# Reordering the first two experts of a mixture-of-experts layer, with an early load of ScalarE's Silu table

## The chip, the cores and the metric

One core of a Trainium2 chip runs the whole program. The metric is the device time of one execution, in microseconds. The program uses TensorE (PE in the profile, PEld for its weight loads), VectorE (DVE), ScalarE (ACT), GpSimd (POOL) and the queues that issue transfers, SyncE's (SP) above all.

## What is computed

One layer: a bidirectional gated linear attention (GLA) over 512 latent tokens with a 256-token context prefix, then a top-2 mixture of 16 experts, then a norm. Cut to what matters here:

```python
x = x + g1 * gla_mixer(modulate(rmsnorm(x), sh1, sc1), ...)
# inside the mixer: the gates of both directions
logdecay = log_sigmoid(z) / 16
# the mixture
scores = sigmoid(h @ w_router)
for e in range(16):
    he = silu(h @ w1[e]) * (h @ w3[e])
    out = out + gates[:, e:e + 1] * (he @ w2[e])
x = x + g2 * out
return rmsnorm(x, final_g)
```

The norms take 1/sqrt through a logarithm and an exponential (`rsqrt`, L139 and L140), and log_sigmoid is made from an absolute value, an exponential and a logarithm (`gate`, L369 to L371).

## The kernel before, in words

The attention part comes first. `rsqrt` normalizes three row blocks of the input (u = 0, 1, 2); TensorE transposes them (L202). Then `proj` runs five projections: for each, weights arrive in the `st` buffers, ScalarE casts them to a rounded copy `wh` (L281), VectorE subtracts to get the rest `wl` (L282), and TensorE does three matmuls per product (`mm3`, L51 to L53). During two of the projections a background generator `gates` is advanced. Each of its 12 steps is a TensorE matmul into a bank of the two-bank pool `pb` (L380 or L385), three ScalarE activations on one tile (L369 Abs, L370 Exp, L371 Ln) and a VectorE operation (L372) that reads the bank again and thereby frees it. So a step's matmul waits for the L372 of the step two before it.

Functions of ScalarE come in table sets. The program's builder puts a table load (ACT_TABLE_LOAD) in front of every activation whose function is not in the set loaded last, and `S.preload_act_table_set` asks for a set by hand. L60 asks for one with both Exp and Ln at the start of the program; L585 and L590 switch for Tanh and back; L1152, the first Silu, has a load in front of it.

Then the output projection, the second norm and the routing: VectorE forms the residual rows (L722, L723), TensorE transposes them (L730) and multiplies the router's weights (L737), and VectorE picks groups, ranks tokens and writes the order of the experts, `eid`, at L1057 (`eidl`). Gate weights are computed on GpSimd by `weights()` (L1083 to L1095) and copied by ScalarE (L1096).

The experts follow in a fixed list `order`; expert 0 is the class `First`, whose rows are collected by a matmul, expert 1 is a `Tile_`, whose rows GpSimd gathers (L1107). `up` computes gate and up products in two halves "a" and "b", `act` the Silu, `tr` and `dn` the down projection, `store` the scaled result, `scatter` the add into memory. `conv` splits weights (ScalarE L56, VectorE L57, 128x1024 each). `release` gives weight buffers back and `pump` issues the next expert's loads on SP.

Who sets the order: outside `manual_schedule` blocks a scheduler places each engine's instructions. In the main loop of the experts only GpSimd (`G.engine`) keeps the written order; TensorE, VectorE and ScalarE are scheduled. `tc.issue_after(ins)` adds an order edge to `ins` for those instructions of its block that run on the engine of `ins`. The weight splits of expert 1's half "a" carry such edges behind `scored[0]` (ScalarE, L909) and `eidl` (VectorE, L1057), at L1258 to L1260. Instructions that need no data and carry no edge can be placed at any point.

Of the kernel before, what the change touches and what calls it, by code (L numbers as in the profile page):

```python
# [32 lines left out]
def dit_kernel(ctx: ExitStack, tc: tile.TileContext, I, out):  # L33
    nc = tc.nc
    V, S, G, PE = nc.vector, nc.scalar, nc.gpsimd, nc.tensor
# [14 lines left out]
    def mm3(o, ah, al, bh, bl, first, last):  # L50
        PE.matmul(o, ah, bh, start=first, stop=False)  # L51
        PE.matmul(o, ah, bl, start=False, stop=False)  # L52
        return PE.matmul(o, al, bh, start=False, stop=last)  # L53
# [136 lines left out]
    for u in range(3):  # L190
# [5 lines left out]
        for k2 in range(4):  # L196
            pt = bank()
            ptv = pt.rearrange("p (k t) -> p k t", k=2)
            for k in range(2):
                for n in range(2):  # L200
                    kt = 2 * k2 + k
# [74 lines left out]
    def conv(st):  # L276
        w = cvs.pop(0)
        cvs.append(w)
        if halves[0]:
            for k in range(2):  # L280
                S.copy(w[0][:, k], st[:, k])  # L281
                mark[0] = V.tensor_sub(w[1][:, k], st[:, k], w[0][:, k].bitcast(F32))  # L282
        else:
            mark[0] = split(w[0], w[1], st)
        return w
# [394 lines left out]
    wts = [{} for _ in range(NE)]  # L680
# [23 lines left out]
    def release(u, *us):  # L704
        free.extend(u.pop(s) for s in us)
        pump()
# [39 lines left out]
    for k2 in range(4):  # L746
        w = first[k2] if k2 < 2 else wconv(2 * k2)
# [11 lines left out]
    w = [wconv(8), wconv(10)]  # L759
# [314 lines left out]
    def ranked():  # L1074
        zz = big1[:, 0:4 * ND * ND].rearrange("p (t a b) -> p t a b", t=4, a=ND)
        V.tensor_mul(zz, zk.unsqueeze(2).to_broadcast([P, 4, ND, ND]), perm.unsqueeze(1).to_broadcast([P, 4, ND, ND]))
        V.tensor_reduce(zk, zz, axis=AX.X, op=OP.add)
        V.tensor_scalar(rv[:, :, NS:NE, 8], zk, 1000.0, None, op0=OP.is_gt)
        V.scalar_tensor_tensor(zp, rv[:, :, NS:NE, 8], -1024.0, zk, op0=OP.mult, op1=OP.add)

    def weights():
        wsel, wsum, gate = big2[:, 256:384].rearrange("p (k t e) -> p k t e", k=2, t=4), R("wsum", [4]), R("gate", [2, 4])
        G.tensor_mul(wsel, oh, sc.unsqueeze(1).to_broadcast([P, 2, 4, NE]))  # L1083
        for n in (8, 4, 2, 1):
            G.tensor_add(wsel[:, :, :, 0:n], wsel[:, :, :, 0:n], wsel[:, :, :, n:2 * n])
        wk = wsel[:, :, :, 0]
        G.tensor_add(wsum, wk[:, 0], wk[:, 1])
        with tc.issue_after(last.ins):
            V.reciprocal(wsum, wsum)
        G.tensor_mul(gate, wk, wsum.unsqueeze(1).to_broadcast([P, 2, 4]))  # L1090
        gsp = R("gsp", [2, 3, 4], BF16)
        for s in range(3):
            G.tensor_copy(gsp[:, :, s], gate)
            if s < 2:
                G.tensor_sub(gate, gate, gsp[:, :, s])  # L1095
        S.copy(rv[:, :, :, 2:8], gsp.rearrange("p k s t -> p t (k s)").unsqueeze(2).to_broadcast([P, 4, NE, 6]))  # L1096
        S.copy(rv[:, :, 0:NS, 8], oh[:, 1, :, 0:NS])
# [30 lines left out]
    class Tile_:  # L1128
# [33 lines left out]

        def dn(s, kt, w):
            for a in range(2):
                mm3(s.py[a], s.hh[:, kt], s.hl[:, kt], w[0][:, a], w[1][:, a], kt == 0, kt == 3)

        def store(s):
            s.y = y = mo.tile([P, D], F32, tag="t4", name="y", bufs=NY)[0:s.w]
            for a in range(2):
                sl = slice(a * 512, a * 512 + 512)  # L1170
                s.mark = V.scalar_tensor_tensor(y[:, sl], s.py[a], s.gs, g2b[0:s.w, sl], op0=OP.mult, op1=OP.mult)  # L1171
# [72 lines left out]
    class Expert:  # L1244
# [32 lines left out]
        def down(s, u):  # L1277
            s.turn()
            for kt in range(4):
                w = u[4 + kt // 2][:, kt % 2 * D:kt % 2 * D + D]  # L1280
                if not s.raw:
                    ws = conv(w.rearrange("p (a n) -> p a n", a=2))
                for t in s.tls:
                    t.dn(kt, w if isinstance(t, Part) else ws)
                if kt % 2:
                    release(u, 4 + kt // 2)
            for t in s.tls:
                t.store()
            s.mark = s.tls[-1].mark
# [11 lines left out]
    def pump():  # L1301
        while queue and free:
            i, s = queue.pop(0)
            if i not in regs:
                p_ = order[i] - NS
                regs[i] = nc.values_load(eid[0:1, p_:p_ + 1], engines=[nc.sync.engine], min_val=0, max_val=NE - 1)
            load_unit(wts[i], regs[i], s)

    def index_for(g):
        c0 = cols[order[g[0]]][0][0]  # L1310
        c1 = cols[order[g[-1]]][-1][0] + 1
        index_of(c0, tiles[c0:c1], lambda e: zp[:, :, e - NS], vals, wide=g[0] == 2)
# [83 lines left out]

    with tc.manual_schedule(engines={G.engine}):
        ex = [Expert(cols[order[0]], True)]
        ex.append(Expert(cols[order[1]]))
        weights()  # L1400
        ranked()
        for i in range(NE - 1):
            ex[i].up(wts[i], "a")
            if i == 1:
                with tc.issue_after(ex[1].tls[0].last.ins):
                    rest()
                    index_for(range(2, 4))
            while i and len(ex) < min(NE, i + 3):
                ex.append(Expert(cols[order[len(ex)]]))
            if i:  # L1410
                ex[i - 1].down(wts[i - 1])
            ex[i].up(wts[i], "b")
            if i % 2 and i + 3 < NE:
                index_for(range(i + 3, min(i + 5, NE)))
            if i:
                ex[i - 1].scatter()
# [118 lines left out]
```

## Time and profile before

| | |
|---|---|
| median of 3 runs | 670.34 us (669.28 to 670.77) |
| profiled execution | 670.26 us |
| its span | 668.5 us |
| mean granted clock of TensorE | 0.976 |
| PE busy | 615.7 us (92%) |
| DVE busy | 467.5 us (70%) |
| ACT busy | 303.3 us (45%) |
| table loads on ACT | 5, 1283 ns each |
| DMA | 170.92 MB, mean 256 GB/s |

Busy shares are means over stages with different limits, so a stage's own windows and waits decide. The span is the time on the core that the profile covers; the profiled execution took 1.8 us more than it.

### The profile page before, as it was taken

The page shows a single profiled execution, that of the slowest core. Times are in us where ns is not written, and L with a number is a line of the kernel's source. Part 1 is how long each engine was busy: PE and PEld are TensorE (multiplying, and loading weights), DVE is VectorE, ACT ScalarE, POOL GpSimd, SP SyncE. Part 2 cuts the span into 40 slices and gives each one's busy share as a digit, 9 for nine tenths or more (in the row PEclk, how much of TensorE's full clock was granted, in tenths as well). Part 3 has the DMA queues.
Part 4 walks back from the last instruction along what each step waited for, and adds up shares of the span by engine and source line. Part 5 has one row for each costly group of instructions (what it writes and reads, how often), then busy time and mean ns, then how long its engine had stood idle before and what let it go on. Part 6 is the DMA issues. An engine that isn't in the chain of part 4 may idle for free. (4 is left out here: it accounts for less than half of the span.)

```text
span 668.5 us, 11368 instructions
## 1 busy us (share of the span) xinstructions
PE 615.7 (92%) x4260; PEld 417.2 (62%) x4260; DVE 467.5 (70%) x994; ACT 303.3 (45%) x513; POOL 102.1 (15%) x104
## 2 busy tenths in 40 slices
PE   3999999999999999999979799999999999999841
PEld 3777677777878878878756565445455557664310
DVE  5776599659958944663687498455576679999615
ACT  6434497276242425623431454243335356773132
POOL 3030000010100010004000153002212222223031
PEclk9999999999999999999989899999999999999975
DMA  8995562110326753387856989999999999999994
GB/s 273 340 352 191 196 245 64 65 64 3 128 71 229 258 201 121 132 312 275 299 190 206 352 283 341 387 345 272 325 358 371 358 337 363 370 371 366 302 343 173
DMA packets 79164, 170.92 MB, mean 256 GB/s; under 512 B 6326, under 2 KB 16876, under 8 KB 78211
## 3 DMA queue, kind: packets, MB, share of 16 engines
q1 hardware_dynamic: 71760, 156.26, 65.8%
q0 software_dynamic: 5248, 10.68, 7.1%
q10 hardware_dynamic: 2098, 3.24, 1.5%
q8 instruction: 34, 0.56, 0.4%
q14 instruction: 24, 0.19, 0.1%
HBM read 158.90 MB, written 13.09 MB: 257 GB/s over the span
## 5 line engine op out<-in xcount | busy, mean ns | idle before, releaser
L51 PE MATMUL bk<-wh,fh 128*128 128x512 f32 (+3 forms) x276 | 111.9, 412 | 1.3 <-ACT fh L56 1.2
L52 PE MATMUL bk<-wl,fh 128*128 128x512 f32 (+3 forms) x276 | 111.1, 404 | 0.3 <-DVE wl L282 0.3
L53 PE MATMUL bk<-wh,fl 128*128 128x512 f32 (+3 forms) x276 | 109.4, 401 | 0.0
L282 DVE TENSOR_TENSOR wl<-st,wh 128x512 fp32r<-128x512 f32 x60 | 39.9, 687 | 39.1 <-ACT wh L281 37.8
L1111 POOL DMA_INDIRECT accd<-y,gix x17 | 40.6, 2390 | 168.4 <-DVE y L1171 78.6
L56 ACT CAST wh<-su 128x1024 fp32r<-128x1024 f32 x45 | 46.8, 1049 | 42.8 <-PE bk L53 41.6
L51 PEld LDWEIGHTS bk<-wh,fh 128*128 128x128 f32 (+3 forms) x276 | 50.4, 184 | 24.2 <-issue 5.9
L281 ACT CAST wh<-st 128x512 fp32r<-128x512 f32 x60 | 35.9, 620 | 61.0 <-PE bk L53 50.9
L57 DVE TENSOR_TENSOR wl<-su,wh 128x1024 fp32r<-128x1024 f32 x45 | 54.5, 1221 | 12.4 <-ACT wh L56 10.7
L52 PEld LDWEIGHTS bk<-wl,fh 128*128 128x128 f32 (+3 forms) x276 | 50.8, 184 | 15.7 <-issue 2.4
L53 PEld LDWEIGHTS bk<-wh,fl 128*128 128x128 f32 (+3 forms) x276 | 50.7, 184 | 13.4 <-issue 1.2
L1207 PE MATMUL bk<-su,xg 128*32 128x256 f32 (+1 forms) x248 | 40.6, 477 | 1.5 <-DVE xg L1201 1.5
L1107 POOL DMA_INDIRECT xg<-h2d,gix x17 | 21.4, 1256 | 87.6 <-DVE ohx L996 49.4
L56 ACT CAST fx<-su 128x1024 fp32r<-128x1024 f32 x21 | 22.0, 1048 | 27.4 <-PE bk L53 27.2
L57 DVE TENSOR_TENSOR fx<-su,fx 128x1024 fp32r<-128x1024 f32 x21 | 25.6, 1221 | 12.0 <-ACT fx L56 11.8
L51 PE MATMUL bk<-fx,fh 128*128 128x512 f32 (+3 forms) x68 | 28.6, 420 | 0.4 <-ACT fh L56 0.4
L1207 PE MATMUL bk<-su,he 128*64 128x512 f32 (+1 forms) x136 | 22.3, 526 | 6.6 <-DMA su<-in_w_down_e_dram 4.6
L52 PE MATMUL bk<-fx,fh 128*128 128x512 f32 (+3 forms) x68 | 27.6, 405 | 0.7 <-DVE fx L57 0.7
L53 PE MATMUL bk<-fx,fl 128*128 128x512 f32 (+3 forms) x68 | 27.2, 401 | 0.2 <-DVE fl L57 0.2
L250 POOL DMA_DIRECT2D mrd<-mrow x8 | 3.8, 487 | 129.7 <-DVE mrow L248 129.7
L1207 PEld LDWEIGHTS bk<-su,xg 128*32 128x32 f32 (+1 forms) x248 | 11.5, 120 | 18.6 <-issue 14.8
L1238 DVE SCALAR_TENSOR_TENSOR y<-bk,gsl,g1b 64x512 f32<-64x512 f32 (+1 forms) x16 | 10.9, 682 | 14.6 <-PE bk L1207 14.5
(478 smaller groups left out, 1321.2 us busy)
## 6 DMA issues: line engine op xcount, KB each, us to landing
su<-in_w_up_e_dram SPq DMA_DIRECT2D x23, 1024.0 KB, 9.0
su<-in_w_down_e_dram SPq DMA_DIRECT2D x21, 1024.0 KB, 7.8
su<-in_w_gate_e_dram SPq DMA_DIRECT2D x19, 1024.0 KB, 7.8
st<-in_gla_w_in_dram SPq DMA_DIRECT2D x10, 1024.0 KB, 6.2
QQ<-in_w_mod_dram SPq DMA_DIRECT2D x5, 1024.0 KB, 7.0
st<-in_w_gate_e_dram SPq DMA_DIRECT2D x5, 1024.0 KB, 8.2
st<-in_w_up_e_dram SPq DMA_DIRECT2D x5, 1024.0 KB, 7.4
B<-in_w_mod_dram SPq DMA_DIRECT2D x4, 1024.0 KB, 4.7
```

The costliest lines, as they stand in the source:

```text
L51: PE.matmul(o, ah, bh, start=first, stop=False)
L52: PE.matmul(o, ah, bl, start=False, stop=False)
L53: return PE.matmul(o, al, bh, start=False, stop=last)
L56: S.copy(hi, full)
L57: return V.tensor_sub(lo, full, hi.bitcast(F32))
L250: G.dma_start(mrd[4 * h_ + c4:4 * h_ + c4 + 1, :], mrow[32 * c4:32 * c4 + 1, :])
L281: S.copy(w[0][:, k], st[:, k])
L282: mark[0] = V.tensor_sub(w[1][:, k], st[:, k], w[0][:, k].bitcast(F32))
L1107: G.indirect_dma_start(out=xg, out_offset=None, in_=src, in_offset=bass.IndirectOffsetOnAxis(ap=idx, axis=0), bounds_check=n - 1, oob_is_e ...
L1111: G.indirect_dma_start(out=dst, out_offset=bass.IndirectOffsetOnAxis(ap=idx, axis=0), in_=y, in_offset=None, bounds_check=n - 1, oob_is_er ...
L1207: PE.matmul(o[s.w * a:s.w * a + s.w], l, r(a), start=first, stop=last, tile_position=(0, s.w * a))
L1238: s.mark = V.scalar_tensor_tensor(y[q], s.py[q], s.gs[q], g2b[q, a * s.n:a * s.n + s.n], op0=OP.mult, op1=OP.mult)
```

## The change

Expert 0's down projection is written before expert 1's gate and up products (its result is stored after the index computation of the next experts); the gate weights are computed on GpSimd before expert 1's gather; and a load of the set `silu_and_others` is asked for inside an `issue_after` behind `eidl`.

```diff
             for a in range(2):
-                mm3(s.py[a], s.hh[:, kt], s.hl[:, kt], w[0][:, a], w[1][:, a], kt == 0, kt == 3)
+                s.last = mm3(s.py[a], s.hh[:, kt], s.hl[:, kt], w[0][:, a], w[1][:, a], kt == 0, kt == 3)
...
                 if kt % 2:
                     release(u, 4 + kt // 2)
+            if s is not ex[0]:
+                s.store()
+
+        def store(s):
             for t in s.tls:
                 t.store()
             s.mark = s.tls[-1].mark
...
         ex = [Expert(cols[order[0]], True)]
+        weights()
         ex.append(Expert(cols[order[1]]))
-        weights()
         ranked()
+        with tc.issue_after(eidl.ins):
+            S.preload_act_table_set("silu_and_others")
         for i in range(NE - 1):
-            ex[i].up(wts[i], "a")
             if i == 1:
-                with tc.issue_after(ex[1].tls[0].last.ins):
+                ex[0].down(wts[0])
+                with tc.issue_after(ex[0].tls[0].last.ins):
                     rest()
                     index_for(range(2, 4))
+                ex[0].store()
+            ex[i].up(wts[i], "a")
             while i and len(ex) < min(NE, i + 3):
                 ex.append(Expert(cols[order[len(ex)]]))
-            if i:
+            if i > 1:
                 ex[i - 1].down(wts[i - 1])
             ex[i].up(wts[i], "b")
```

How the engines' instructions move is told below by the built programs' own order (line, operation, destination and sources; a line of the changed kernel lies up to 8 further down: its L1407 is the new preload).

The first place is ScalarE, at two points. One is the start of its program, up to the first of the three `rsqrt` calls (`sg` belongs to the conditioning vector, `fl` to the sums of squares).

```order
 L60 ACT_TABLE_LOAD
+L1407 ACT_TABLE_LOAD
+L114 ACT_TABLE_LOAD
 L114 ACTIVATE sg<-cc 128x16
 L192 ACTIVATE fl,ss_138<-KK 128x1024 x2
+L139 ACT_TABLE_LOAD
 L139 ACTIVATE rsl<-ss_138,epsc 128x2
+L140 ACT_TABLE_LOAD
 L140 ACTIVATE rstd_137<-rsl 128x2
```

The new preload stands directly behind L60, at the start of the program: ScalarE's instructions get no edge from `eidl`, which runs on VectorE. Each L139 and L140 of the three calls now has a load in front of it.

The other point is ScalarE during the gates (`E_87` holds a step's values, `wh_485` a cast weight). Before:

```order
L369 ACTIVATE E_87<-bk 128x512
L370 ACTIVATE E_87<-E_87 128x512
L371 ACTIVATE E_87<-E_87 128x512
L369 ACTIVATE E_87<-bk 128x512
L281 CAST wh_485<-st 128x512
L370 ACTIVATE E_87<-E_87 128x512
L369 ACTIVATE E_87<-bk 128x512
```

and now:

```order
L369 ACTIVATE E_87<-bk 128x512
L370 ACTIVATE E_87<-E_87 128x512
L371 ACT_TABLE_LOAD
L371 ACTIVATE E_87<-E_87 128x512
L369 ACTIVATE E_87<-bk 128x512
L281 CAST wh_485<-st 128x512
L370 ACT_TABLE_LOAD
L370 ACTIVATE E_87<-E_87 128x512
```

From the first L371 to the last L417 (an Exp behind the gates) 24 loads are added in this way. The load at L585 is gone, those at L590, L1152 and L1448 (L1440 before) stay.

The second place is VectorE ahead of the routing (`su_2694` and `su_2695` hold expert 0's down weights, `srg` the residual rows, `he` a transposed copy for the router).

```order
 L829 TENSOR_SCALAR rsv<-ss_2742 128x1
+L57 TENSOR_TENSOR wl_486<-su_2694,wh_485 128x1024
 L835 TENSOR_SCALAR lss<-rstd_2743,rsv 128x1
 L836 TENSOR_SCALAR lss<-lss 128x1
+L57 TENSOR_TENSOR fx<-su_2694,fx 128x1024
 L837 TENSOR_TENSOR rstd_2743<-rstd_2743,lss 128x1
 L722 TENSOR_TENSOR srg<-bk,g1b 128x512
+L57 TENSOR_TENSOR wl_488<-su_2695,wh_487 128x1024
 L723 TENSOR_TENSOR srg<-srg,su_2692 128x512
```

Three weight splits of expert 0's down projection now stand among the last residual rows. They have no edge behind `eidl`; three splits of expert 1's weights, which stood behind `eidl` before, are no longer early.

The third place is TensorE where expert 0's gate and up products end (`full` holds its rows, `xg` expert 1's gathered rows, `he` expert 0's Silu product, `fh` and `fl` rounded rows and rest). Before:

```order
L1186 MATMUL bk<-su_2699,full 128x512
L1141 MATMUL bk<-ident,xg 128x128 x8
L51 MATMUL bk<-fx,fh 128x512
L52 MATMUL bk<-fx,fh 128x512
L51 MATMUL bk<-wh_485,fh 128x512
L52 MATMUL bk<-wl_486,fh 128x512
L1159 MATMUL bk<-ident,he 128x128
```

and now:

```order
L1186 MATMUL bk<-su_2699,full 128x512
L1159 MATMUL bk<-ident,he 128x128 x4
L51 MATMUL bk<-fx,fh 128x512
L52 MATMUL bk<-fx,fh 128x512
L53 MATMUL bk<-fx,fl 128x512 x2
```

Expert 0's transposes and its 24 down matmuls come first; expert 1's transposes (L1141) follow after them and some index matmuls (L1019, L1002). On GpSimd the 11 instructions of `weights()` move from behind expert 1's gather to ahead of it, and nothing else there changes its place.

## Rows read from the trace of the kernel before

**Rows 1.** Page, part 2: busy tenths in 40 slices of 16.7 us.

```profile
PE   3999999999999999999979799999999999999841
...
ACT  6434497276242425623431454243335356773132
```

**Rows 2.** Busy time of each engine in three stretches, with clock and DMA.

```profile
core 0: us, PE busy (x) PEld busy (x) DVE busy (x) ACT busy (x) POOL busy (x), PEclk, DMA share, GB/s
30.00:60.00 30.00, 30.00 (x289) 23.27 (x279) 22.61 (x50) 11.08 (x21) 5.96 (x12) 1.00 0.94 308
60.00:80.00 20.00, 20.00 (x125) 12.59 (x124) 7.95 (x10) 6.91 (x13) 1.46 (x2) 1.00 0.49 166
80.20:110.20 30.00, 28.66 (x125) 22.46 (x124) 28.23 (x35) 26.80 (x51) 0.00 (x0) 1.00 0.49 169
```

**Rows 3.** ACT in order of time (start us, us) around two table loads.

```profile
228.83 1.28 ACT L585 ACT_TABLE_LOAD   x1
231.54 2.70 ACT L585 ACTIVATE srg<-bk 128x512 f32<-128x512 f32 x4 [1.43 <-PE bk L53]
...
257.87 1.28 ACT L590 ACT_TABLE_LOAD   x1
259.16 0.62 ACT L281 CAST wh<-st 128x512 fp32r<-128x512 f32 x1
```

**Rows 4.** ACT, DVE and PE in order of time in the first 20 us.

```profile
11.25 1.06 ACT L192 ACTIVATE fl<-A 128x1024 fp32r<-128x1024 f32 x1 [1.49 <-DMA A<-in_x_dram]
...
16.23 0.20 ACT L140 ACTIVATE rstd<-rsl 128x2 f32<-128x2 f32 x1
...
16.46 0.16 DVE L127 TENSOR_TENSOR rst<-rstd 128x2 f32<-128x2 f32 x1 [0.15 <-ACT rstd L140]
...
19.28 0.74 PE L202 MATMUL bk<-ident,QQ 128*128 128x128 f32 x4
```

**Rows 5.** ACT from 80 to 116 us: its waits, one group, two neighbours.

```profile
ACT E L369 <- PE bk L385: 2.3, 2, 1.6
ACT E L369 <- PE bk L380: 0.4, 1, 0.4
...
L371 ACT ACTIVATE E<-E 128x512 f32<-128x512 f32 x12 | 7.6, 634 | 0.1
...
84.96 0.63 ACT L371 ACTIVATE E<-E 128x512 f32<-128x512 f32 x1
85.48 0.63 ACT L370 ACTIVATE E<-E 128x512 f32<-128x512 f32 x1
```

**Rows 6.** DVE ahead of the routing in order of time; a weight-split group.

```profile
336.89 0.69 DVE L722 TENSOR_TENSOR srg<-bk,g1b 128x512 f32<-128x512 f32 x1
...
339.13 0.69 DVE L732 COPY he<-bk 128x512 f32<-128x512 f32 x1 [0.81 <-PE bk L730]
...
L57 DVE TENSOR_TENSOR fx<-su,fx 128x1024 fp32r<-128x1024 f32 x21 | 25.6, 1221 | 12.0 <-ACT fx L56 11.8
```

**Rows 7.** PE, ACT and DVE where expert 1 starts; busy time there.

```profile
372.75 1.09 PE L1141 MATMUL bk<-ident,xg 128*128 128x128 f32 x8 [2.64 <-DMA xg<-h2d,gix]
374.19 0.80 PE L51 MATMUL bk<-fx,fh 128*128 128x512 f32 x1 [0.35 <-ACT fh L56]
...
383.53 0.50 PE L51 MATMUL bk<-wh,fh 128*128 128x512 f32 x1 [1.16 <-ACT fh L56]
...
371.23 0.52 ACT L1096 COPY rv<-gsp 128x384 bf16<-128x384 bf16 x1 [12.26 <-POOL gsp L1093]
...
373.06 0.60 ACT L1152 ACTIVATE he<-bk 128x512 f32<-128x512 f32 x1
...
373.69 0.69 DVE L1153 TENSOR_TENSOR he<-he,bk 128x512 f32<-128x512 f32 x1 [4.11 <-ACT he L1152]
...
374.00:376.00 2.00, 1.81 (x4) 1.40 (x5) 1.58 (x3) 0.63 (x2) 0.00 (x0) 0.50 1.05 385
...
380.00:390.00 10.00, 8.85 (x56) 6.57 (x55) 9.95 (x28) 5.92 (x8) 2.45 (x2) 1.00 0.69 238
```

## The prediction, made before the changed kernel was run

> **What bounds the kernel now.** I read the 40 slices first [rows 1]: TensorE shows nines from slice 1 almost to the end, so whatever holds it up anywhere before the experts is paid in full, unless something later gives it back. In slices 5 and 6 ScalarE is at 9 and 7 as well; that is the stretch of the gates. The windows say how much room there is [rows 2]: TensorE is busy for all of 30 to 80 us, and in 80.2 to 110.2 us ScalarE is busy for 26.80 us of 30, VectorE for 28.23 and TensorE for 28.66. Three engines are nearly full there, and the one that is given more work sets the pace. Then I read the neighbours of a table load on ScalarE [rows 3], the first 20 us [rows 4], ScalarE's own waits in the gates [rows 5], VectorE ahead of the routing [rows 6], and the start of expert 1 [rows 7].
>
> **What the change does in fact.** The preload's edge is behind an instruction of VectorE and does not bind ScalarE, so the order has it at the start of the program. From there on the set with both Exp and Ln is no longer the one loaded last, and each change between the two gets a load: L1407 and L114, six at L139 and L140, 24 in and behind the gates, 32 in all; one, at L585, goes. The table load of L1152, for whose sake it was written, stays.
>
> **The price of one load.** It is 1.28 us, and the loads do not overlap their neighbours: the load at 257.87 is followed by a cast at 259.16 [rows 3]. In a dense stretch two neighbours do overlap, with starts 0.52 us apart at a length of 0.63 [rows 5], so a load between two such neighbours takes 0.11 us more. The Trainium skill ("ScalarE: Activation LUTs", What ACT_TABLE_LOAD costs) adds a drain of about 1.38 us to the load's 1.283, some 2.66 us for each switch. The cast at 259.16 speaks against it in this trace, and the sum by it is given with the rivals.
>
> **The start: +6.5 us.** The first two new loads fall while ScalarE still waits for the first input block; I cost them at nothing, and without that cover they are 2.6. The other six stand in the three `rsqrt` chains, whose last one ends with the Exp at 16.23; VectorE takes it up 0.15 us later, and TensorE's transposes of the third block at 19.28 hang on that [rows 4]. Six loads are 7.7; ScalarE's wait of 1.49 us for the input at 11.25 [rows 4] swallows that much; three lost overlaps add 0.3. So 6.5 us. Since TensorE then is full to 80 us [rows 2], it has nothing to give back. The ends are 3 (VectorE and TensorE find work meanwhile) and 8.
>
> **The gates: +30 us.** ScalarE has 24 loads more between 82 and 110 us: 24 x 1.283 = 30.8. In 18 places they part neighbours that overlap: 18 x 0.11 = 2.0. ScalarE's waits of 2.3 and 0.4 us in this stretch [rows 5] are swallowed: -2.7. That gives 30.1. Can TensorE go on meanwhile? It has weights cast ahead, but its gate matmuls sit among the others in order and each waits for a bank that the L372 of the step two before frees, and so for ScalarE's L371. It stops at each of them and loses a piece each time. Behind the last step come an Exp of four parts (L417), whose transposes TensorE needs, and the Exp at L476, so the whole delay arrives. VectorE runs the same steps in order and cannot get ahead either. The ends are 24 (PE, DVE or a prefetched transfer make up for some waits later) and 34.
>
> **The load that goes: 0.** Behind the load at 228.83 ScalarE waits 1.43 us for TensorE [rows 3]. Without it the wait is longer.
>
> **TensorE's clock: +2 us.** After the idle 2.64 us before 372.75 the clock granted in 374 to 376 us was 0.50, the 1.2 GHz level, so 2 us of work took as long as 1 at the full level [rows 7]. At the start and behind the gates TensorE idles for some 6 us each; I take 1 us of loss for each. The ends are 0 (the short gaps hide it) and 4.
>
> **Ahead of the routing: +3.5 us.** Three splits of 1.22 us on VectorE [rows 6] now stand between L829 and L723, with casts before them on ScalarE that must wait for TensorE's last use of the buffers. VectorE ran L722 at 336.89, and the next steps for the router follow with a wait of 0.81 us [rows 6] that is itself the answer of TensorE to L723. So nothing covers them: 3.7, less a little overlap, 3.5. They delay the router and with it `eid`, on which all later weight loads wait. What they replace stood in idle time. The ends are 1 and 5.
>
> **Expert 0 and 1: -2 us.** Before, TensorE waited 2.64 us for the gather, 0.35 for a cast and 1.16 for expert 0's cast, and lost 1.0 by the clock [rows 7]: 5.2 in all. Now the gate weights come first on GpSimd and in the time before the gather, so L1096 no longer holds ScalarE until 371.23, and the load that is still in front of the first Silu runs before TensorE is done. Silu (0.60) and product (0.69) [rows 7] follow at once: 1.3 us of wait, then two casts as at 374.19, 0.35 each, so 2.0, and perhaps the clock's 1.0. This leaves a gain of 2.2 to 3.2. VectorE, though, is busy for 9.95 us of 380 to 390 [rows 7], with the same number of splits to do, and may keep part of it. I take 2.0; the ends are 0 and 4. On SP the same loads follow in the same order of experts. They start as buffers are given back, and expert 0's down buffers, split early, come free no later than before.
>
> **The sum.** 6.5 + 30.1 + 2 + 3.5 - 2 = 40.1 us on the profiled execution's 670.26 us, which agrees with the median of 670.34 to 0.1. I forecast **710 us**.
>
> **Rivals.**
> *Faster: the loads lie in slack.* If ScalarE's extra 40 us ran beside other work, TensorE working from weights already cast, only the experts' part would count: 670.3 - 3 = 667, with the splits hidden as well. It decides by ScalarE's idle time in the gates: from about 31 us on nothing is lost, and the windows show 3.2 [rows 2]. I give 3%.
> *Each switch costs 2.7.* The one row in which nothing follows a load at once is L585: from 228.83 to 231.54 are 2.71 us [rows 3]. If that is a drain and not the wait for TensorE that the profile names, each of the 30 loads in the chains costs 1.43 us more: 43 us, for 753. The cast at 259.16 and the Silu that starts at 373.06, behind L1096's end at 371.75 and one load [rows 7], speak against it. This is the sum by the Trainium skill's rule as well, nearly. I give 5%.
> *It does not do what the order shows.* If the loads were dropped or the preload ran late, the routing's 3.5 and the experts' -2 remain: 672. I give 2%.
> *Given back later.* If waits of ScalarE or VectorE behind the gates vanish, as TensorE finds their work done, 8 to 15 us return: 695 to 702. The trace has no engine that could run ahead, but transfers do. I give 15%, of which half lies in the range below.
>
> **How the numbers follow.** My own case, 75%, spans 698 to 717 by the ends of its terms, which will not all fall on one side. Range 698 to 717: it leaves out the faster rival, the drain, the preload that is late, and the lower half of what is given back, about 18 in 100. A measurement of this kernel can tell about 0.2%, 1.3 us. Faster by that: 0.03, the first rival. The same: 0.01, from the third. Slower: 0.96.
>
> **What would show it.** Right: 36 table loads on ScalarE, the third Exp of L140 near 23 us, TensorE idle before the gate matmuls L385 by 2 to 3 us a time with L372 named, ScalarE without a gap from about 87 to 150 us, L1057 later by some 42 us, and the wait of 2.64 us before L1141 gone. Wrong: a load that is followed by more than 1.4 us of nothing (the drain), TensorE busy through the gates (slack), or a last third that is shorter than before by more than 3 us (given back).

## The result, and the profile after

The changed kernel takes 709.92 us (median of 4 runs, 709.19 to 711.69) beside 669.86 us for the kernel before on the same chip: a ratio of 1.0593 [1.0567, 1.0619]. The profiled execution took 709.32 us against 670.26, 39.1 us more; its span is 707.5 us. The forecast was 710.

The 40 slices of the changed kernel, 17.7 us each, answer to [rows 1]:

```profile
PE   2899976679999999999997989999999999999861
...
ACT  8633399961854214363244235433334447774132
```

TensorE, at nine before, is at 7, 6, 6 and 7 in slices 5 to 8, and ScalarE is at 9, 9, 9 and 6 there. ScalarE is the engine that sets the pace in the gates now. The windows say the same; the first answers to the second line of [rows 2], the second is the stretch of the gates (columns as in [rows 2]):

```profile
30.00:60.00 30.00, 30.00 (x289) 22.42 (x290) 20.73 (x58) 9.78 (x21) 5.97 (x12) 1.00 0.90 297
...
86.00:156.00 70.00, 49.47 (x226) 35.73 (x225) 36.83 (x46) 64.03 (x81) 0.00 (x0) 0.80 0.27 90
```

In 70 us of the gates ScalarE is busy for 64.03, TensorE for 49.47. How ScalarE spends it is seen in its instructions in order of time, where a load stands in front of every change between Exp (L370) and Ln (L371):

```profile
93.88 1.28 ACT L371 ACT_TABLE_LOAD   x1
95.18 0.63 ACT L371 ACTIVATE E<-E 128x512 f32<-128x512 f32 x1
95.82 1.28 ACT L370 ACT_TABLE_LOAD   x1
97.12 0.63 ACT L370 ACTIVATE E<-E 128x512 f32<-128x512 f32 x1
```

Two thirds of such a piece is loading. The activation starts 1.29 or 1.30 us after its load did, so nothing but the load itself lies between. The groups of instructions by line count the loads (busy us and mean ns of one behind the bar):

```profile
L371 ACT ACT_TABLE_LOAD x12 | 15.4, 1283 | 0.2
L370 ACT ACT_TABLE_LOAD x10 | 12.8, 1283 | 0.2
L139 ACT ACT_TABLE_LOAD x3 | 3.8, 1283 | 0.1
L140 ACT ACT_TABLE_LOAD x3 | 3.8, 1283 | 0.1
L417 ACT ACT_TABLE_LOAD x2 | 2.6, 1283 | 0.0
```

With L60, L1407, L114, L590, L1152 and L1448 these are 36. TensorE's longest waits between 86 and 156 us (us in total, times, longest) name VectorE's L372, which stands behind ScalarE's Ln, and at L423 ScalarE's last Exp, L417:

```profile
PE bk L385 <- DVE AA L372: 7.8, 4, 2.9
PE bk L423 <- ACT E L417: 4.8, 3, 3.4
PE bk L385 <- DVE GBc L372: 3.4, 1, 3.4
PE bk L380 <- DVE AA L372: 2.3, 1, 2.3
```

Behind the last of these loads TensorE transposes what L417 gave (L423), and in the changed kernel the Exp at L476 starts 0.08 us after the last of these transposes is over. The windows from the first L423 behind L417's last two parts to the end of L423, of the kernel before and of the changed one; then ScalarE and TensorE there, in the same order:

```profile
110.20:113.10 2.90, 2.90 (x22) 2.64 (x21) 2.35 (x5) 2.90 (x6) 0.00 (x0) 1.00 0.95 306
...
146.20:151.40 5.20, 5.18 (x19) 4.47 (x20) 2.67 (x4) 3.39 (x6) 0.00 (x0) 0.50 0.01 2
```

```profile
109.48 0.90 ACT L417 ACTIVATE E<-GFc,tot 128x256 f32<-128x256 f32 x2
112.03 1.04 PE L423 MATMUL bk<-ident,E 128*128 128x128 f32 x8
113.31 1.91 ACT L476 ACTIVATE E<-AA 128x2048 f32<-128x2048 f32 x1
...
145.66 0.91 ACT L417 ACTIVATE E<-GFc,tot 128x256 f32<-128x256 f32 x2
149.46 1.91 PE L423 MATMUL bk<-ident,E 128*128 128x128 f32 x8
151.45 1.92 ACT L476 ACTIVATE E<-AA 128x2048 f32<-128x2048 f32 x1 [1.86 <-issue]
```

After a wait of 3.43 us (at 146.22, the longest of the L423 row above) the granted clock is 0.50 there, the 1.2 GHz level, where the kernel before had 1.00. Eight transposes take 1.91 us in place of 1.04, and from L417's last parts to L476 it is 5.8 us in place of 3.8.

The routing on VectorE answers to [rows 6]; the three splits now stand here, and L732 starts at 381.17 in place of 339.13:

```profile
375.07 1.22 DVE L57 TENSOR_TENSOR wl<-su,wh 128x1024 fp32r<-128x1024 f32 x1
...
376.73 1.23 DVE L57 TENSOR_TENSOR fx<-su,fx 128x1024 fp32r<-128x1024 f32 x1
...
378.54 1.22 DVE L57 TENSOR_TENSOR wl<-su,wh 128x1024 fp32r<-128x1024 f32 x1
379.67 0.69 DVE L723 TENSOR_TENSOR srg<-srg,su 128x512 f32<-128x512 f32 x1
381.17 0.69 DVE L732 COPY he<-bk 128x512 f32<-128x512 f32 x1 [0.81 <-PE bk L730]
```

The start of the experts answers to [rows 7]; ScalarE, then TensorE:

```profile
406.22 1.28 ACT L1152 ACT_TABLE_LOAD   x1
410.85 0.60 ACT L1152 ACTIVATE he<-bk 128x512 f32<-128x512 f32 x1 [3.35 <-PE bk L1186]
...
412.53 0.66 PE L1159 MATMUL bk<-ident,he 128*128 128x128 f32 x4 [0.85 <-DVE he L1153]
413.86 0.50 PE L51 MATMUL bk<-fx,fh 128*128 128x512 f32 x1 [0.68 <-ACT fh L56]
...
419.84 1.07 PE L1141 MATMUL bk<-ident,xg 128*128 128x128 f32 x8
```

The wait for the gather is gone, and the load, still in front of the first Silu, is over 3.35 us before the Silu's input is there.

Where the time went is read by the start of the same instruction in each kernel. The table has it for all the kernels of this study (us from the span's start, by the source line of the kernel before; e1 to e9 are the experiments below):

| | third Exp L140 | Exp L476 | VectorE L732 | first L1186 | first Silu L1152 | last Silu L1152 | span |
|---|---|---|---|---|---|---|---|
| before | 16.2 | 113.3 | 339.1 | 356.1 | 373.1 | 604.0 | 668.5 |
| after | 22.6 | 151.5 | 381.2 | 397.7 | 410.9 | 643.7 | 707.5 |
| e1 no preload | 15.9 | 112.7 | 341.9 | 358.5 | 371.7 | 604.6 | 672.3 |
| e2 preload alone | 22.6 | 150.5 | 376.6 | 392.5 | 410.0 | 641.0 | 705.7 |
| e3 preload tied | 15.9 | 113.0 | 342.1 | 358.7 | 371.8 | 604.7 | 669.5 |
| e4 splits tied, no preload | 16.2 | 113.8 | 339.4 | 355.3 | 368.4 | 601.6 | 667.6 |
| e4 once more | 16.0 | 113.3 | 339.1 | 355.1 | 368.3 | 601.4 | 667.3 |
| e5 gates only | 15.9 | 137.4 | 364.3 | 380.9 | 394.0 | 627.0 | 695.3 |
| e6 start only | 22.4 | 120.0 | 346.9 | 363.6 | 376.7 | 609.6 | 674.0 |
| e7 down projection only | 16.3 | 114.2 | 339.8 | 357.0 | 373.8 | 609.3 | 674.6 |
| e8 the same, preload tied | 16.3 | 113.2 | 339.0 | 356.0 | 371.7 | 605.8 | 671.7 |
| e9 gate weights only | 16.1 | 113.0 | 338.8 | 355.6 | 368.8 | 603.7 | 669.8 |

Read across the second line: 6.4 us late at the third Exp, 38.1 at L476 behind the gates (151.45 and 113.31), 42.0 at L732, 41.6 at L1186, 39.7 at the last Silu, 39.0 at the end. Each line is one execution, up to 1.8 us off its kernel's median; e1 and e3 agree in their medians and differ here behind the last Silu alone.

### The profile page after: what moved, and what is told of

Same layout as the page of the kernel before. It is cut to its first block, busy times and chain, and to the rows that moved or that the text cites. A ratio compares the mean times of both kernels' runs of the same rounds, so it can differ in the third digit from the quotient of the medians.

```text
span 707.5 us, 11397 instructions
## 1 busy us (share of the span) xinstructions
PE 630.8 (89%) x4260; PEld 424.5 (60%) x4260; DVE 468.2 (66%) x994; ACT 344.3 (49%) x544; POOL 102.4 (14%) x104
## 5 line engine op out<-in xcount | busy, mean ns | idle before, releaser
L51 PE MATMUL bk<-wh,fh 128*128 128x512 f32 (+3 forms) x276 | 113.0, 417 | 0.8 <-ACT fh L56 0.4
L1111 POOL DMA_INDIRECT accd<-y,gix x17 | 38.5, 2265 | 167.8 <-DVE y L1171 79.7
L1107 POOL DMA_INDIRECT xg<-h2d,gix x17 | 22.6, 1327 | 43.1 <-DVE pis L1010 15.2
L53 PE MATMUL bk<-fh,wl 128*128 128x512 f32 x48 | 20.9, 435 | 0.0
```

What stands on the lines that cost most here:

```text
L1107: G.indirect_dma_start(out=xg, out_offset=None, in_=src, in_offset=bass.IndirectOffsetOnAxis(ap=idx, axis=0), bounds_check=n - 1, oob_is_e ...
L1111: G.indirect_dma_start(out=dst, out_offset=bass.IndirectOffsetOnAxis(ap=idx, axis=0), in_=y, in_offset=None, bounds_check=n - 1, oob_is_er ...
```

## The experiments

The theory: nearly all of the 39 us is the 32 added table loads, which come from the preload's place and from nothing else; the moved down projection costs 3 us in the routing and gives 2 to 3 back in the experts. The rivals: the loads are cheap and the moved down projection is what costs; or each load costs more than its own 1.28 us.

**e1, without the preload.**

```diff
         ranked()
-        with tc.issue_after(eidl.ins):
-            S.preload_act_table_set("silu_and_others")
         for i in range(NE - 1):
```

> The change without its preload; expert 0's down projection ahead of expert 1 and the gate weights first stay. Theory (the 32 added table loads cost 38 to 39 us, the routing's three splits 3, the experts' part gives 2 to 3 back): 5 table loads, no wait of ScalarE in the gates that was not there before, L732 about 3 us later than in the kernel before, the end at 669 to 672 us. Rival A (the loads are cheap, most of the 40 us comes from the down projection that was moved): 690 us or more. Rival B (the early splits stand in idle time and only the experts' gain counts): 666 to 668 us.

Measured: 672.58 us, 0.6 above the expected range, a ratio of 1.002 [0.9997, 1.0043]; five loads; L732 2.8 us late. Rivals A and B of the expectation fall: without the preload the kernel is within 0.4% of the one before. What a load costs this run does not say; e5 does.

**e2, the preload alone**, put into the kernel before.

```diff
         ranked()
+        with tc.issue_after(eidl.ins):
+            S.preload_act_table_set("silu_and_others")
```

> The kernel before with the preload of the Silu table alone. Theory: the preload is at the start of the program, 36 table loads, 706 to 710 us, and L476 later by about 38 us as in the changed kernel. Rival (the loads cost less by themselves and the moved down projection makes up the difference): under 700 us.

Measured: 709.17 us, 1.0578 [1.0534, 1.0623]; 36 loads; L476 37.2 us late, and 37.2 late at the end of the span. So the preload alone costs what the whole change costs, and what is lost by L476 is still lost at the end: nothing is given back over the 550 us that follow.

**e3, the preload tied to an instruction of ScalarE.**

```diff
-        with tc.issue_after(eidl.ins):
+        with tc.issue_after(scored[0].ins):
             S.preload_act_table_set("silu_and_others")
```

> The changed kernel with the preload tied to the Exp of L909, an instruction of ScalarE, in place of the copy of VectorE. Theory: 5 loads, one of them between that Exp and the first L972, none in front of the first Silu. Since the load at L1152 is already over before TensorE is done with expert 0, the time is that of the version without the preload within 0.7 us. Rival A (that load is on the path to Silu): faster than the version without the preload by 1.3 us. Rival B (in its new place it holds up L972, and through L969 everything behind): slower by 0.7 to 1.3 us.

Measured: 672.27 us, 1.0019 [0.9998, 1.004], beside e1's 1.002. ScalarE in order of time, e3:

```profile
345.58 0.26 ACT L909 ACTIVATE sc<-lg 128x64 f32<-128x64 f32 x1 [1.80 <-DVE lg L862]
345.86 1.28 ACT L1407 ACT_TABLE_LOAD   x1
355.10 1.50 ACT L972 ACTIVATE full<-bk,m2T 128x128 f32<-128x128 f32 x4 [7.96 <-PE bk L969]
```

Now the load stands in a wait of some 9 us. It costs nothing, and it gains nothing, because the gate weights put first have already moved the other load out of the Silu's way. The instruction that the edge names is worth 5.7% of the time (1.0593 against 1.0019).

**e4, without the preload, the down projection's splits tied behind the routing.**

```diff
                 if not s.raw:
-                    ws = conv(w.rearrange("p (a n) -> p a n", a=2))
+                    with ExitStack() as cc:
+                        if s is ex[0]:
+                            for i in [scored[0], eidl]:
+                                cc.enter_context(tc.issue_after(i.ins))
+                        ws = conv(w.rearrange("p (a n) -> p a n", a=2))
```

> As the version without the preload, and the three splits for expert 0's down projection that had moved in between the steps of the routing are tied behind it (behind L909 on ScalarE and L1057 on VectorE). Theory: L732 is back at its time of the kernel before, 3 us earlier than without the tie, and the experts' part keeps its gain: 666 to 668.5 us. Rival (the splits are then late for the down projection, and TensorE waits for them behind the first Silu as it did for expert 1 before): the 3 us come back there and the time is 669 to 671 us.

> The version without the preload and with the down projection's splits tied behind the routing, once more, as the yardstick of the three runs that follow. Theory: a ratio to the kernel before of 0.995 to 0.999, as in the first measurement. Rival (that was chance): a ratio of 1.000 to 1.003.

Measured: 669.54 us, 0.9974 [0.9954, 0.9994], and again 668.8 us, 0.9978 [0.9955, 1.0]. The first time lies in the rival's range (669 to 671) and above the theory's (666 to 668.5); the second run's ratio is within what was expected. This version is faster than the changed kernel, and than the kernel before by some 0.2%, though the second interval ends at 1.0. The routing's 3 us are back (L732 at 339.4), so the rival's reason, 3 us of waiting for the splits, is not what the trace shows; TensorE goes on from expert 0's Silu without the gather, with a wait of 0.68 for a cast, e4:

```profile
370.11 0.66 PE L1159 MATMUL bk<-ident,he 128*128 128x128 f32 x4 [0.85 <-DVE he L1153]
371.44 0.50 PE L51 MATMUL bk<-fx,fh 128*128 128x512 f32 x1 [0.68 <-ACT fh L56]
...
377.43 1.07 PE L1141 MATMUL bk<-ident,xg 128*128 128x128 f32 x8
```

At the last Silu it is 2.4 us ahead of the kernel before, at the end only 0.8. Of the 2.4, 0.8 is there at the first L1186 already. In 346 to 356 us the granted clock was 1.00 in e4 and 0.83 in the kernel before, and e2, which has that kernel's code there, had 1.00 as well in the like stretch; so this part need not come from the change. The 1.6 us lost behind the last Silu go near the end of the program, where TensorE waits for weights. One group of 32 matmuls ahead of that wait takes 1.93 us in the kernel before and 3.88 in e4, where the granted clock is 0.59. But e4's second profile has the clock at 1.00 in that place and 2.42 us for the group, and ends 1.2 us ahead, not 2.4. The group's window and the wait, of the kernel before, of e4, and the window of e4 once more:

```profile
635.00:637.40 2.40, 1.93 (x32) 0.94 (x32) 0.36 (x1) 1.76 (x5) 0.29 (x1) 1.00 0.99 300
```

```profile
639.71 0.67 PE L1207 MATMUL bk<-st,xg 128*32 128x256 f32 x4 [2.36 <-DMA st<-in_w_gate_e_dram]
```

```profile
633.00:637.00 4.00, 3.88 (x32) 2.01 (x32) 0.00 (x0) 1.39 (x4) 1.56 (x1) 0.59 1.03 329
```

```profile
638.54 0.62 PE L1207 MATMUL bk<-st,xg 128*32 128x256 f32 x4 [1.64 <-DMA st<-in_w_gate_e_dram]
```

```profile
632.50:637.00 4.50, 2.42 (x32) 1.05 (x32) 0.26 (x1) 1.66 (x5) 1.33 (x1) 1.00 1.02 315
```

At the next wait, for `in_w_up_e_dram`, TensorE goes on at 642.37 in the kernel before, at 641.70 in e4 and at 641.50 in its second profile: leads of 0.7 and 0.9 us. By these rows it is the landing of the last experts' weights that sets the time there, whatever the clock ahead of it; no run was made on those transfers themselves.

**e5, the loads in the gates only, and e6, those at the start only.** In e5 the preload is tied to the last cast of L343, in e6 the set with Exp and Ln is loaded again ahead of the gates.

```diff
+        gmark = S.copy(lowT[:, o0:o0 + n], pl[:, 0:n])
...
-        with tc.issue_after(eidl.ins):
+        with tc.issue_after(gmark.ins):
             S.preload_act_table_set("silu_and_others")
```

```diff
+    tc.keep_in_program_order(S.preload_act_table_set("natural_log_exp_and_others"))
     ps = proj(0, True, False, False, budget=4.8, mods=[m2b[0:1], m2b[::-1], m2b[::-1], m2b[::-1]])
```

> The changed kernel with the preload tied to the last cast of L343 on ScalarE, behind the start and ahead of the gates. The scheduler pairs some steps of the gates, so that 21 loads stand at L370, L371 and L417, and one at L1407 ahead of them. Theory (each load 1.28 us of ScalarE, paid in full in the gates): 22 x 1.28 = 28.2 less the 2.7 us of waits that they swallow, 25.5 us over the version without the preload, 695 to 699 us, and the first 70 us as in the kernel before. Rival A (a drain with each switch, 2.7 us): 720 us or more. Rival B (the start cost most of it): under 688 us.

> The changed kernel with the preload where it was, at the start of the program, and the set that holds both Exp and Ln loaded again ahead of the gates (L404). Theory: 8 loads at the start, none in the gates; the third Exp of L140 near 22.6 us in place of 16.2, the lag of 6 to 7 us stays through TensorE's full stretch, 677 to 680 us. Rival A (TensorE gives it back before the gates): within 2 us of the version without the preload, 670 to 674 us. Rival B (what follows from TensorE's idle time and its clock at the start costs as much again): 682 us or more.

Measured: e5 695.99 us, 1.0366 [1.0323, 1.0408]; e6 677.63 us, 1.0095 [1.0063, 1.0128]. The expectation for e5 counted 22 loads; the trace has 20 more than the kernel before in and ahead of the gates: nine each at L370 and L371, one at L417 and one at L1407. The one at L1407 (72.23) stands in a wait ahead of the gates, whose first L369 starts no later than before (80.28 and 80.63). The other 19 are 24.4 us, less 2.7 for the waits 21.7; the last row of L417 ends 22.8 us late (133.23 and 110.38), L476 starts 24.1 late. With rival A's 2.7 us for each it would be some 49 us. TensorE waits for the banks of L385 and L380 again, 13.2 us in all. In e6 there is no load in the gates, and most of what is late at the start stays late. ScalarE in order of time and the window of 15 to 30 us, e6:

```profile
22.41 0.20 ACT L140 ACTIVATE rstd<-rsl 128x2 f32<-128x2 f32 x1
...
120.01 1.92 ACT L477 ACTIVATE E<-AA 128x2048 f32<-128x2048 f32 x1
```

```profile
15.00:30.00 15.00, 12.13 (x107) 9.75 (x105) 10.36 (x34) 11.92 (x21) 0.00 (x0) 1.00 1.12 336
```

L477 of e6 is L476 of the others: 6.7 us late (the load at L404 stands ahead of the gates as well), and the third Exp 6.2. These two kernels are no pure addition to e1, though: in both, TensorE has six matmuls fewer in the trace between L476 and L590 than e1, and that stretch takes 142.1 and 142.2 us in place of 144.5. Against e1, which has the same routing, e5 is 22.4 us late at L732 and e6 5.1, and so they stay to the last Silu.

**e7, e8 and e9, the parts of the rest.** e7 is e4 with the gather ahead of the gate weights again; e8 is e7 with the preload tied as in e3; e9 is the kernel before with the gate weights first.

```diff
         ex = [Expert(cols[order[0]], True)]
-        weights()
         ex.append(Expert(cols[order[1]]))
+        weights()
```

> That version with the gather ahead of the gate weights on GpSimd again, so that of the change only the moved down projection is left. Theory (the gate weights hold ScalarE's L1096, and so the load and the first Silu): L1096 near 371.2 us, the load behind it, the first Silu near 373 us in place of 368.4, TensorE without work from 370 to 374.7, and the last expert stages some 4 us later than in the yardstick; the end at 671 to 674 us. Rival (the down projection moved is enough, since the Silu only waits for TensorE): within 0.7 us of the yardstick.

> As the run above, with the preload of the Silu table tied to the Exp of L909 on ScalarE. Theory: here the load stands in front of a Silu on which TensorE waits, so the preload takes one load off the path: the first Silu 1.28 us earlier, near 371.8 us, and the end 0.5 to 1.3 us below the run above. Rival (the load's new place holds up L972 as much as its old one held up the Silu): no difference.

> The kernel before with the gate weights ahead of the gather on GpSimd, and nothing else. Theory (GpSimd stands idle for the weights' time before the gather's indices are there, so that the gather is issued at the same time; the first Silu is earlier, but TensorE has expert 1 in front of expert 0's down projection and waits for its gather as before): the wait of 2.6 us before L1141 stays, the first Silu near 370.7 us, and the time is that of the kernel before within 0.8 us. Rival A (the gather slips by the weights' 4.5 us): slower by 3 us or more. Rival B (the early Silu is what gives the experts' gain): faster by 2 us.

Measured: e7 675.66 us, 1.007 [1.0044, 1.0095]; e8 673.24 us, 1.0032 [1.0015, 1.0049]; e9 672.01 us, 1.0015 [0.9995, 1.0036]. ScalarE and TensorE of e7 in order of time, and the window behind the wait (columns as in [rows 2]):

```profile
371.94 0.52 ACT L1096 COPY rv<-gsp 128x384 bf16<-128x384 bf16 x1 [12.09 <-POOL gsp L1093]
372.49 1.28 ACT L1152 ACT_TABLE_LOAD   x1
373.78 0.60 ACT L1152 ACTIVATE he<-bk 128x512 f32<-128x512 f32 x1
...
375.15 1.11 PE L1159 MATMUL bk<-ident,he 128*128 128x128 f32 x4 [4.17 <-DVE he L1153]
```

```profile
375.00:385.00 10.00, 9.17 (x35) 7.01 (x36) 3.50 (x5) 3.75 (x4) 0.00 (x0) 0.66 0.82 287
```

The same of e8:

```profile
371.25 0.53 ACT L1096 COPY rv<-gsp 128x384 bf16<-128x384 bf16 x1 [12.39 <-POOL gsp L1093]
371.68 0.59 ACT L1152 ACTIVATE he<-bk 128x512 f32<-128x512 f32 x1
...
373.04 0.66 PE L1159 MATMUL bk<-ident,he 128*128 128x128 f32 x4 [3.04 <-DVE he L1153]
```

And TensorE and GpSimd of e9:

```profile
372.91 1.77 PE L1141 MATMUL bk<-ident,xg 128*128 128x128 f32 x8 [3.33 <-DMA xg<-h2d,gix]
...
366.15 1.59 POOL L1107 DMA_INDIRECT xg<-h2d,gix  x1 [0.73 <-issue]
```

The moved down projection alone is slower than the kernel before: TensorE now has nothing ahead of the Silu's result, and on ScalarE the Silu stands behind L1096, which waits for GpSimd's gate weights. The gate weights alone gain nothing: the first Silu is 4.3 us earlier, 1.9 more than expected, and TensorE still waits 3.33 us for the gather. Only together (e4) do they gain. The gather loses nothing by standing second: it is issued at 366.15 in e9, and at 366.2 in the kernel before, where GpSimd stood idle in front of it. What it waits for then is not settled; the changed kernel's row names the write of `h2d`. In e8 a tied preload does what a preload is for: the Silu follows L1096 with no load in between.

e7 came out 1.7 us above its expected range, and e8's gain over it is 2.4 us where 1.3 was the most expected. The rows show where, for e7: behind the wait of 4.17 us the granted clock was 0.66 over the next 10 us, where e4 had 1.00 for the same work, and from the first L1159 to the first L1141 it took 9.99 us (375.15 to 385.14) in place of e4's 7.32. So to a wait 3.3 us longer than e4's the slower clock added 2.7; the other 1.7 of the 7.7 us between the two at the last Silu are there at L1186. In e8 the wait is 1.1 us shorter than in e7, the clock in 373 to 383 us was 0.83, and the same stretch took 8.60.

## Why the prediction was right

- **What the change does in fact.** As put: 36 loads, L585's gone, L1152's still there. e2 and e3 show it from both sides: the preload alone makes 36, the same call with its edge on ScalarE makes 5.
- **The price of one load, 1.28.** Confirmed at each of the 24 loads in the gates: the next activation starts 1.29 to 1.30 us behind the load's start. The drain of the Trainium skill ("ScalarE: Activation LUTs", What ACT_TABLE_LOAD costs) is not there: by an estimate from that page's 1.38 us, e5 would have been later by another 19 x 1.38 = 26.2 us. The measurement decides.
- **The start, +6.5.** Measured +6.4 at the third Exp and +6.6 at the first L369 of the gates (87.23 against 80.63). e6 has it alone: 6.2 and, at L476, 6.7. TensorE, busy for all of 30 to 80 us in both, gave none of it back there, as the windows had said.
- **The gates, +30.1.** From the first L369 to the last row of L417 the lag grows from 6.6 to 36.2 us (145.66 and 109.48), so 29.6. TensorE stopped at its gate matmuls with L372 named, up to 2.9 or 3.4 us at a time, as put.
- **TensorE's clock, +2.** The size came out, the places only in part: 1 us was put at the start and 1 behind the gates. At the start nothing is seen of it: e6, with 1.00 in 15 to 30 us, is as late as the changed kernel with 0.89. Behind the gates it is 2.0: from the last row of L417 to L476 the lag grows from 36.2 to 38.1 while TensorE works at 0.50, and e2 has the same (35.2 and 37.2, at 0.50). That the two errors cancel is luck. In the gates the mean was 0.80; there ScalarE sets the pace, and no loss by TensorE's clock was separated.
- **Ahead of the routing, +3.5.** 3.0: L732 on ScalarE ahead of the splits (372.10, 333.12 before) is 39.0 us late, L732 on VectorE 42.0. e1 has 2.8 at that place, e4 takes it back.
- **Experts 0 and 1, -2.** From L1186 to the last Silu the lag falls from 41.6 to 39.7, so -1.9, and to 39.0 at the end. What was not foreseen is that both of its parts are needed for it (e7, e9).
- **The sum, 40.1.** 39.1 measured on the profiled execution. Parts that no term names nearly cancel: +0.9 between L476 and the splits, -0.5 from L732 to L1186, -0.7 behind the last Silu. So the hit on the median to 0.1 us is partly luck; that each large term is right within 0.5 us is not.
- **The rivals.** "Loads in slack" and "each switch costs 2.7" fall by the trace and by e5. "It does not do what the order shows", 672, is what e1 and e3 measure, 672.58 and 672.27: the working for the case without loads was right as well. "Given back later" falls by e2, late by 37.2 us at L476 and at the end.

## What to carry to other kernels

A preload is an instruction without data: it stays in place only if something binds it on its own engine, an edge (e3, e5) or a kept program order (e6). Look in the order at where it stands, and count the table loads before anything is run; where one engine's chain sets the pace, as ScalarE's did here, the count times 1.28 us less its waits is close to the cost (e5: 21.7 by that sum, 22.8 measured in the gates). Of a change in several parts, try each alone and all but one: here one part costs 37 us; of the other two one loses alone and one gains nothing, and together, with the splits kept out of the routing, they gain some 0.2%.

## What the runs showed that was not expected

- The same preload, put behind the start, makes 18 loads at L370 and L371 in place of 22: in e5 the last six of the twelve steps run in pairs, two Exp and then two Ln, and share a load.
- An idle time of TensorE of 4.17 us was followed by a granted clock of 0.66 over 10 us, one of 0.85 us (e4) by 1.00. In e7 a wait 3.3 us longer than e4's cost 6.0 in all, as the next stretch took 2.7 us more. The same stands behind the gates of the changed kernel: 3.43 us of waiting, then 0.50.
- A lead of 2.4 us at the last Silu shrank to 0.8 by the end of e4, and one of 2.6 to 1.2 in its second profile, although the clock there was 0.59 in the one and 1.00 in the other: the waits for the last experts' weights took the rest.
